# Preparing modulation, context and the first tokens by feature block in a hybrid recurrent trunk on one core

## The chip, the core and the metric

The kernel runs on one core of one Trainium2 chip. Its engines run side by side, each on an instruction list of its own: TensorE (PE; its weight loads are listed as PEld), VectorE (DVE), ScalarE (ACT), GpSimd (POOL) and SyncE (SP). SP and ACT also issue DMA transfers, in the order of their lists. The metric is the device time of one execution in microseconds. Three runs of the kernel before gave a median of 2798.66 us (2794.95 to 2799.27).

## The reference, cut to what matters

One layer: an HGRN2 gated recurrence over 2048 latent tokens of 1024 features, preceded by 256 context tokens that share all weights, then a gated ConvFFN. The change lies in the first steps, the modulated norm and the projections of the first head.

```python
sc_lat, sc_ctx = jax.nn.silu(c), jax.nn.silu(c_ctx)
m_l = (sc_lat @ w_ada[l] + b_ada[l])[:, None, :]
m_c = sc_ctx @ w_ada[l] + b_ada[l]
sh1, sc1, g1, sh2, sc2, g2 = jnp.split(m_l, 6, axis=-1)
csh1, csc1, ... = jnp.split(m_c, 6, axis=-1)
hl = modulate(rmsnorm(lat, norm_g[l, 0]), sh1, sc1)     # h * (1 + scale) + shift
hc = modulate(rmsnorm(cx, norm_g[l, 0]), csh1, csc1)
# in the mixer, for context and latents alike, 8 heads of 128:
q, zf_fwd, zf_bwd, v, g = jnp.split(h @ w_in, 5, axis=-1)
q = silu(q)
f = lb[d] + (1.0 - lb[d]) * sigmoid(zf)                  # per direction d
logf, k = log(f), 1.0 - f
# chunkwise scan of each direction: S_t = diag(f_t) S_{t-1} + k_t v_t^T, o_t = S_t^T q_t
# the latent scans start from the context's final state
out = (rmsnorm(o, g_gain) * silu(g)) @ w_out
```

After the mixer come the residual, the second modulated norm, the ConvFFN (a depthwise convolution of width 3 between two large products) and the final norm.

## The kernel before, in words

**Number format.** Large products are made from two-term splits: `split` (L76) writes a rounded high part with an ACT copy (L77) and the remainder with a DVE subtraction (L78). A product is then three matmuls (high x high, high x low, low x high).

**Modulation rows (L196 to L220).** The first 2048 columns of w_ada give shift and scale. SP and ACT load them as 16 blocks of 128 x 1024 (0.5 MB each) into four large places of SBUF; later the tokens live in the same places (`place`, L133). Per block two float32 matmuls (L205) with the two silu columns of c and c_ctx as weights write 2 x 512 values into four banks. Each such matmul shows as two instructions in the trace, 64 in all. ACT copies the four banks (L212), 16 small transposes (L215) turn the rows into columns, and DVE makes A1 (scale) and B1 (shift), for latents and context.

**Tokens.** A tile is 128 tokens of 1024 features. `load_x` (L175) loads it (L163) and `normalize` (L93) scales it: a square with sum on ACT (L97), a small DVE operation (L73), a power on POOL (L74), the scaling on ACT (L100). `transpose_mod` (L104) turns four blocks of 128 features on TensorE (L109) into one bank and modulates each on ACT (L113) or DVE (L116), 128 x 128 at a time; `put_tok` (L146) splits the half tile into its place. Two context tiles and token tile 0 are made so at once (L221 to L229). Tiles 1 to 7 follow by `make_tok` (L383), one tile after another through one bank.

**Heads.** Half of the tokens (tiles 0 to 7, two units of four tiles) go through all eight heads, then the other half. `head` (L702) runs for each head: three context projections, of the two gates and the values (L714), and for each unit five projections (two gates, query, value, output gate). A projection (`acc`, L367) has eight steps, one for each block of 128 features, of three matmuls each (L372 to L374), 512 columns wide for a unit and 256 for the context. `gates`, `factors`, `values` and `unit_steps` (L402 to L616) make the scan's factors on ACT, DVE and POOL, and the scores, states and outputs with small matmuls (L503 to L602).

**Order.** The program is traced in the order of the source, and a scheduler with a cost model puts each engine's instructions in a fixed list, mostly in that order, taking ready work earlier where an engine would sit idle. An agenda written by hand (`at`, `tick`, L353 to L365) puts side work behind the n-th projection step: tiles 1 to 4 at steps 2 to 18, tiles 5 to 7 from step 20 on (L773 to L778). `issue_after` puts instructions behind a given one on the same engine's list. A buffer with few copies makes the next user's load wait until the last reader is through; raw weight blocks have two (`rawp`), split weights four (`wp`).

In the first head unit 0's gates, query and value are projected, then unit 1's gates, query and value, then both output gates (L744 to L754).

Of the kernel before, what the change touches and what calls it, by code (L numbers as in the profile page):

```python
# [11 lines left out]
F32 = mybir.dt.float32  # L12
# [33 lines left out]
def body(ctx, tc, a, out):  # L46
# [29 lines left out]
    def split(h, l, src):  # L76
        act.activation(h, src, AF.Copy)  # L77
        dve.tensor_tensor(l, src, h.bitcast(F32), OP.subtract)  # L78
# [67 lines left out]
    def put_tok(hm, t, kh):  # L146

        src = hm[:, 4 * kh:4 * kh + 4]
        j = t % UT
        if t < 0:  # L150
            b = cxt[:, kh, t + 2]
            split(b[:, 0], b[:, 1], src)
        elif t < HT:
            b = block(t // UT, kh)[:, j]
            split(b[:, 0], b[:, 1], src)
        else:
            b = xp.tile([128, 2, 4, 128], F32R, name="stg", tag="stg", bufs=1)
            split(b[:, 0], b[:, 1], src)
            sp.dma_start(tok_d[t // UT - 2][kh][:, j], b.bitcast(F32))
# [15 lines left out]
    def load_x(xt, t, hm=None):  # L175
        x_tile(xt, t)
        junk = hm.rearrange("p k n -> p (k n)") if hm is not None else \
            xp.tile([128, D], F32, name="junk", tag="stg", bufs=1)
        normalize(xt, junk, gp, on_act=True)


    HEAD0 = (2, 1, 3, 0)
    staged = {}
    with ExitStack() as c0:
        p0s = pool_(c0, "p0s", space=PSUM)
        silv = sil.rearrange("p (two k) -> p k two", two=2)
        mps = [p0s.tile([2, 512], F32, name=f"mps{n}") for n in range(4)]
        ada = [place(i, [128, 4, D], F32, "wada") for i in range(4)]

        def early_x(t):  # L190

            tag = ("ke", "ke", "kd", "qp", "qp", "qi", "qi")[t + 2]
            staged[t] = gp.tile([128, D], F32, name="x0", tag=tag, bufs=1 if tag == "kd" else 2)
            load_x(staged[t], t)

        act.activation(sil, vec[:, V_C:V_C + 16], AF.Sigmoid)  # L196
        dve.tensor_tensor(sil, sil, vec[:, V_C:V_C + 16], OP.mult)
        for k in range(KT):
            for i in range(2):
                n = 2 * k + i  # L200
                wt = ada[n // 4][:, n % 4]
                (sp if i else act).dma_start(
                    wt, a["w_ada"][k * 128:(k + 1) * 128, i * D:(i + 1) * D])
                for n in range(2):
                    pe.matmul(mps[2 * i + n], silv[:, k, :], wt[:, n * 512:(n + 1) * 512],  # L205
                              start=k == 0, stop=k == KT - 1)
            if 3 <= k < 6:
                early_x(k - 5)
        head0 = {ty: load_w(0, ty) for ty in HEAD0[:2]}
        m2 = [gp.tile([2, 512], F32, name="m2", tag="qg"[n // 2], bufs=2) for n in range(4)]  # L210
        for n in range(4):
            ada_done = act.activation(m2[n], mps[n], AF.Copy)  # L212
        mt = p0s.tile([128, 16, 2], F32, name="mt")
        for j in range(16):
            pe.transpose(mt[:, j, :], m2[j // 4][:, j % 4 * 128:(j % 4 + 1) * 128],  # L215
                         ident[0:2, 0:2])
        for i in (1, 0):
            dve.tensor_tensor(B1[i], mt[:, 0:8, i], vec[:, V_BA:V_BA + 8], OP.add)
            dve.tensor_tensor(A1[i], mt[:, 8:16, i], vec[:, V_BA + 8:V_BA + 16], OP.add)
            dve.scalar_tensor_tensor(A1[i], A1[i], 1.0, vec[:, V_NG:V_NG + 8], OP.add, OP.mult)  # L220
        hms = [new_hm(),  # L221
               xp.tile([128, KT, 128], F32, name="hm", tag="xt", bufs=1),
               gp.tile([128, KT, 128], F32, name="hm", tag="S", bufs=1)]
        for g in range(2):
            for j, hm in enumerate(hms):
                t = j - 2
                m = 0 if t >= 0 else 1
                transpose_mod(staged[t], hm, g, p0s, A1[m], B1[m], "tr", 3, (g + j) % 2)
                put_tok(hm, t, g)  # L229
        with tc.issue_after(ada_done.ins):  # L230
            head0.update({ty: load_w(0, ty) for ty in HEAD0[2:]})
            for t in range(1, 5):
                early_x(t)
# [75 lines left out]
    def mixer_scan():  # L309
# [56 lines left out]

        def acc(z, w, rs):  # L367

            for k in range(KT):
                r = rs[k // 4]  # L370
                h, l = r[:, :, 0, k % 4], r[:, :, 1, k % 4]
                pe.matmul(z, w[:, 0, k], h, start=k == 0, stop=False, skip_group_check=True)  # L372
                pe.matmul(z, w[:, 0, k], l, start=False, stop=False, skip_group_check=True)  # L373
                pe.matmul(z, w[:, 1, k], h, start=False, stop=k == KT - 1, skip_group_check=True)  # L374
                tick()
# [7 lines left out]
        def make_tok(t, xt=None):  # L383

            got = [xt]
            hms = []
# [6 lines left out]
            def put(g):  # L393
                if not hms:
                    hms.append(new_hm())
# [1199 lines left out]
```

## Time and profile before

| | |
|---|---|
| Median of three runs | 2798.66 us |
| The profiled execution | 2798.74 us, its span 2797.0 us |
| TensorE busy | 2732.9 us (98% of the span) |
| DVE, ACT, POOL busy | 1977.5, 1147.7, 571.9 us |
| DMA | 402.18 MB, mean 144 GB/s |
| Granted clock of TensorE | 0.99 mean |

Rows of a table of stretches give start and end, the length, then for each engine its busy time and number of instructions, then TensorE's granted clock (1.00 is full), the share of time that the DMA engines were busy, and GB/s. Rows of the order in time give start, length, engine, line and operation, what is written from what, the shape, and in brackets how long the engine had been idle and what ended that. Rows of groups give busy time and the mean length of one instruction in ns, then the idle time in front of them. A matmul's length is its own, from entering to leaving; in a stream the next enters before it, so a stream's price is read from start to start. Rows of waits give total, count and the longest.

### The profile page before, as it was taken

To read this page: it belongs to the slowest core of one execution; us is meant where nothing else is said; L and a number is where in the kernel's file an instruction comes from. 1 tells how busy PE (TensorE), PEld (TensorE's weight loads), DVE (VectorE), ACT (ScalarE), POOL (GpSimd) and SP (SyncE) were. 2 spreads that over 40 slices of the span, in tenths; PEclk is the share of its full clock that TensorE was granted. 3 is DMA by queue.
4 is the path that set the end of the run, shared out by engine and by line. 5 is a ranking of instruction groups with operands and counts; after the bars stand their busy time and mean duration, and the time that the engine had idled before them with its cause. 6 is when DMAs were issued, how large, how long until landed. Compare 5 with 4: busy or idle time off the path is not lost. (4 is left out here: it accounts for less than half of the span.)

```text
span 2797.0 us, 42007 instructions
## 1 busy us (share of the span) xinstructions
PE 2732.9 (98%) x16072; PEld 2269.1 (81%) x16072; DVE 1977.5 (71%) x2804; ACT 1147.7 (41%) x1908; POOL 571.9 (20%) x882
## 2 busy tenths in 40 slices
PE   7899999999999999998999999999999999999998
PEld 3688888888888888886887788888888888887887
DVE  3665556657575775567887877887877787576886
ACT  5423343323233332324666444444444444333343
POOL 2211111111111111111120443432344430000001
PEclk9999999999999999998999999999999999999999
DMA  5122333215442432236888422226222223987663
GB/s 227 54 62 86 95 114 100 86 54 172 165 129 71 129 106 76 84 110 233 284 306 309 149 85 81 91 91 266 95 90 77 91 91 122 328 290 242 197 195 121
DMA packets 226161, 402.18 MB, mean 144 GB/s; under 512 B 29220, under 2 KB 136612, under 8 KB 222120
## 3 DMA queue, kind: packets, MB, share of 16 engines
q1 hardware_dynamic: 221928, 390.79, 42.0%
q10 hardware_dynamic: 4032, 8.72, 0.8%
q8 instruction: 126, 2.06, 0.3%
q14 instruction: 75, 0.61, 0.1%
HBM read 289.04 MB, written 110.38 MB: 143 GB/s over the span
## 5 line engine op out<-in xcount | busy, mean ns | idle before, releaser
L372 PE MATMUL z<-tok,w 128*128 128x512 f32 x1280 | 516.4, 404 | 0.0
L374 PE MATMUL z<-tok,w 128*128 128x512 f32 x1280 | 502.5, 393 | 0.0
L373 PE MATMUL z<-tok,w 128*128 128x512 f32 x1280 | 501.5, 392 | 0.0
L78 DVE TENSOR_TENSOR w<-raw,w 128x512 fp32r<-128x512 f32 (+1 forms) x260 | 239.6, 925 | 146.8 <-ACT w L77 142.8
L374 PEld LDWEIGHTS z<-tok,w 128*128 128x128 f32 x1280 | 241.3, 189 | 51.2
L372 PEld LDWEIGHTS z<-tok,w 128*128 128x128 f32 x1280 | 242.3, 189 | 47.3 <-issue 3.5
L373 PEld LDWEIGHTS z<-tok,w 128*128 128x128 f32 x1280 | 242.1, 189 | 44.5
L77 ACT ACTIVATE w<-raw 128x512 fp32r<-128x512 f32 (+1 forms) x260 | 196.1, 760 | 134.0 <-PE zd L857 77.4
L1427 PE MATMUL y<-wd,ml 128*128 128x512 f32 x600 | 234.8, 391 | 3.7 <-DVE ml L78 3.7
L1425 PE MATMUL y<-wd,mh 128*128 128x512 f32 x600 | 234.1, 390 | 1.2 <-ACT X L1460 1.2
L1426 PE MATMUL y<-wd,mh 128*128 128x512 f32 x600 | 233.9, 390 | 0.0
L426 DVE TENSOR_TENSOR_SCAN S<-F,d 128x528 f32<-128x528 f32 (+1 forms) x80 | 91.6, 1145 | 99.9 <-ACT F L409 99.3
L78 DVE TENSOR_TENSOR w<-s,w 128x512 fp32r<-128x512 f32 x126 | 121.0, 965 | 54.5 <-ACT w L77 53.7
L854 PE MATMUL zc<-rT,w 128*128 128x512 f32 x352 | 137.1, 390 | 1.2 <-DVE uv L1312 1.0
L857 PE MATMUL zc<-rT,w 128*128 128x512 f32 x352 | 136.9, 389 | 0.0
L856 PE MATMUL zc<-rT,w 128*128 128x512 f32 x352 | 136.9, 389 | 0.0
L1427 PEld LDWEIGHTS y<-wd,ml 128*128 128x128 f32 x600 | 113.0, 188 | 29.0 <-DVE ml L78 5.8
L77 ACT ACTIVATE w<-s 128x512 fp32r<-128x512 f32 x126 | 78.3, 628 | 138.8 <-POOL s L910 82.2
L1425 PEld LDWEIGHTS y<-wd,mh 128*128 128x128 f32 x600 | 113.1, 188 | 25.0 <-ACT X L1460 1.7
L459 POOL COPY TX<-S 128x4 f32<-128x4 f32 x32 | 25.1, 784 | 529.0 <-DVE S L426 529.0
L1426 PEld LDWEIGHTS y<-wd,mh 128*128 128x128 f32 x600 | 112.9, 188 | 23.7
L854 PE MATMUL za<-rB,w 128*128 128x512 f32 x336 | 130.7, 389 | 0.0
(339 smaller groups left out, 6334.1 us busy)
## 6 DMA issues: line engine op xcount, KB each, us to landing
raw<-in_w_up_dram SPq DMA_DIRECT2D x88, 512.0 KB, 3.9
raw<-in_w_in_dram SPq DMA_DIRECT2D x80, 512.0 KB, 3.8
lr<-m SPq DMA_DIRECT2D x49, 512.0 KB, 5.7
m<-r SPq DMA_DIRECT2D x66, 256.0 KB, 4.2
spare<-in_w_ada_dram SPq DMA_DIRECT2D x32, 512.0 KB, 4.5
kq<-stash SPq DMA_DIRECT2D x15, 1024.0 KB, 7.8
og<-stash SPq DMA_DIRECT2D x28, 512.0 KB, 5.2
u<-in_w_down_dram SPq DMA_DIRECT2D x51, 256.0 KB, 3.9
```

The lines of the kernel that those rows point to most:

```text
L77: act.activation(h, src, AF.Copy)
L78: dve.tensor_tensor(l, src, h.bitcast(F32), OP.subtract)
L372: pe.matmul(z, w[:, 0, k], h, start=k == 0, stop=False, skip_group_check=True)
L373: pe.matmul(z, w[:, 0, k], l, start=False, stop=False, skip_group_check=True)
L374: pe.matmul(z, w[:, 1, k], h, start=False, stop=k == KT - 1, skip_group_check=True)
L426: dve.tensor_tensor_scan(flat(S[:, d]), flat(F[:, d]), flat(d1[:, 0:ns]), 0.0, OP.mult, OP.max)
L854: pe.matmul(o, w[:, 0, k], r[:, :, 0, k], start=start and k == 0, stop=False, skip_group_check=True)
L856: pe.matmul(o, w[:, 0, k], r[:, :, 1, k], start=False, stop=False, skip_group_check=True)
L857: pe.matmul(o, w[:, 1, k], r[:, :, 0, k], start=False, stop=k == 3, skip_group_check=True)
L1425: pe.matmul(z, lh, rh, start=start, stop=False, skip_group_check=True)
L1426: pe.matmul(z, lh, rl, start=False, stop=False, skip_group_check=True)
L1427: pe.matmul(z, ll, rh, start=False, stop=stop, skip_group_check=True)
```

## The change

**Rows.** The silu columns are copied into a zeroed tile `silp` of 32 columns per feature block. For each block k four matmuls write 32 partitions each of one bank `mp`: shift in two halves, scale in two halves. One ACT copy and four transposes of 128 x 128 follow. Two w_ada blocks (k of 6 and 7) move from SP's queue to ACT's. Raw weights of the two gates are loaded between the w_ada blocks, those of value and query behind the first two token tiles.

**Context.** Both context tiles are normalized with the scaling on DVE (`on_act` is left out) and transposed before the modulation rows are ready, into four banks of two feature blocks by two tiles. Modulation is then 128 x 256 at a time, and each quarter is split at once.

**Tokens of units 0 and 1.** All eight tiles are loaded into buffers of their own (`stage`), which later serve the scan, and normalized in place with a common junk tile. `unit_tok` transposes one feature block of all four tiles of a unit into one of three banks in turn, modulates 128 x 512 at a time (even blocks on ACT, odd ones on DVE) and splits. Three blocks of unit 0 stand in the third context projection. Then both gates of unit 0 advance together, block by block, each step followed by the block three ahead; the agenda puts the squares of tiles 4 to 7 and the blocks of unit 1 among these steps and the query's. `make_tok` is left for the other half's tiles.

```diff
     def split(h, l, src):
-        act.activation(h, src, AF.Copy)
-        dve.tensor_tensor(l, src, h.bitcast(F32), OP.subtract)
+        i = act.activation(h, src, AF.Copy)
+        j = dve.tensor_tensor(l, src, h.bitcast(F32), OP.subtract)
+        return i.ins, j.ins
+    @contextmanager
+    def behind_of(pair):
+        with tc.issue_after(pair[0]), tc.issue_after(pair[1]):
+            yield
...
+    def stage(t):
+        tag = ("ke", "ke", "qp", "qp", "qi", "qi", "xt", "hm", "stg", "raw")[t + 2]
+        p = {"xt": xp, "hm": xp, "stg": xp, "raw": rawp}.get(tag, gp)
+        staged[t] = p.tile([128, D], F32, name="x0", tag=tag, bufs=1 if p is xp else 2)
+        x_tile(staged[t], t)
+    def turn_tok(tp, ts, ks):
+        for i, k in enumerate(ks):
+            for j, t in enumerate(ts):
+                pe.transpose(tp[:, i, j], staged[t][:, k * 128:(k + 1) * 128], ident)
+    def modulated(hm, tp, k, m, on_act):
+        if on_act:
+            act.activation(hm, tp, AF.Identity, bias=B1[m][:, k:k + 1], scale=A1[m][:, k:k + 1])
+        else:
+            dve.tensor_scalar(hm, tp, A1[m][:, k:k + 1], B1[m][:, k:k + 1], OP.mult, OP.add)
...
+        pool.memset(silp, 0.0)
+        for k in range(2):
+            ada_load(act, k, 0)
+            ada_load(sp, k, 1)
         act.activation(sil, vec[:, V_C:V_C + 16], AF.Sigmoid)
         dve.tensor_tensor(sil, sil, vec[:, V_C:V_C + 16], OP.mult)
+        dve.tensor_copy(silp[:, :, 0:2], silv)
+        stage(-2)
+        stage(-1)
+        for k in range(2, KT):
+            ada_load(act, k, 0)
+            ada_load(act if k >= 6 else sp, k, 1)
+            if k in (4, 5):
+                head_raw[6 - k] = raw_w(6 - k)
+        stage(0)
+        stage(1)
+        for t in (-2, -1):
+            normalize(staged[t], junk, gp)
+        late_junk = place(2, [128, D], F32, "junk")
...
         for k in range(KT):
+            if k == 5:
+                for g in range(4):
+                    turn_tok(tps[g], (-2, -1), (2 * g, 2 * g + 1))
+            for c in range(4):
+                n = 2 * k + c // 2
+                pe.matmul(mp[32 * c:32 * c + 32], silp[:, k],
+                          ada[n // 4][:, n % 4, c % 2 * 512:(c % 2 + 1) * 512],
+                          start=k == 0, stop=k == KT - 1, skip_group_check=True)
+        split_head0(2, head_raw[2])
+        act.activation(m2, mp, AF.Copy)
+        for j in range(4):
+            pe.transpose(mt[:, j], m2[:, j * 128:(j + 1) * 128], ident)
...
+        for g in range(4):
+            hm = gp.tile([128, 2, 2, 128], F32, name="hm", tag="g", bufs=2)
             for i in range(2):
+                modulated(hm[:, i], tps[g][:, i], 2 * g + i, 1, i == 0)
+            b = cxt[:, g // 2, :, :, 2 * (g % 2):2 * (g % 2) + 2]
+            made = split(b[:, :, 0], b[:, :, 1], hm.rearrange("p k s n -> p s k n"))
+            if g == 1:
+                split_head0(1, head_raw[1])
+                with behind_of(made):
+                    normalize(staged[0], late_junk, gp)
+        head_raw[3] = raw_w(3)
+        stage(2)
+        stage(3)
+        head_raw[0] = raw_w(0)
+        for t in range(4, 8):
+            stage(t)
+        with behind_of(made):
+            normalize(staged[1], late_junk, gp)
+            split_head0(3, head_raw[3])
+            for t in (2, 3):
+                normalize(staged[t], late_junk, gp)
...
+        places = ("kv", "o", "tr")
+        def unit_tok(u, k):
+            tp = ps.tile([128, 1, UT, 128], F32, name="tp", tag=places[k % 3], bufs=1)
+            turn_tok(tp, range(UT * u, UT * u + UT), (k,))
+            hm = gp.tile([128, UT, 128], F32, name="hm", tag="g", bufs=2)
+            modulated(hm, tp[:, 0], k, 0, k % 2 == 0)
+            b = block(u, k // 4)[:, :, :, k % 4]
+            return split(b[:, :, 0], b[:, :, 1], hm)
...
                 ckd, csd = factors(h, None, None, None)
+                if first:
+                    made_tok = []
+                    for k in range(3):
+                        at(clock[0] + 2 * k, lambda k=k: made_tok.append(unit_tok(0, k)))
                 cv, turn = values(project(weight(3), None), 2)
...
             if first:
-                gate(0)
+                zs = [ps.tile([128, UT, 128], F32, name="z", tag="pj", bufs=3) for _ in range(2)]
+                def more(t):
+                    with behind_of(made_tok[-1]):
+                        normalize(staged[t], late_junk, gp)
+                for i in range(UT):
+                    at(clock[0] + 1 + 2 * i, lambda i=i: more(UT + i))
+                for k in range(KT):
+                    at(clock[0] + 10 + 2 * k, lambda k=k: unit_tok(1, k))
+                for k in range(KT):
+                    for d, z in enumerate(zs):
+                        step(z, weight(2 - d), block(0, k // 4), k)
+                    if k + 3 < KT:
+                        made_tok.append(unit_tok(0, k + 3))
+                    if k == 3:
+                        split_head0(0, head_raw[0])
+                for d, z in enumerate(zs):
+                    gates(d, h, 0, z)
                 query(0, 24)
...
-        for t in range(1, 5):
-            for i, f in enumerate(make_tok(t, staged[t])):
-                at(2 + 4 * (t - 1) + 2 * i, f)
-        for t in range(5, 8):
-            for i, f in enumerate(make_tok(t)):
-                at(20 + 10 * (t - 5) + 3 * i, f)
```

More of the change, by code (lines that the diff above doesn't have):

```diff
@@ L146, in put_tok @@
     def put_tok(hm, t, kh):
[L148 to L159, printed above, removed]
+        b = xp.tile([128, 2, 4, 128], F32R, name="stg", tag="stg", bufs=1)
+        split(b[:, 0], b[:, 1], hm[:, 4 * kh:4 * kh + 4])
+        sp.dma_start(tok_d[t // UT - 2][kh][:, t % UT], b.bitcast(F32))
     def x_tile(xt, t):
@@ new lines, in ada_load, with raw_w, split_head0 @@
+        def ada_load(q, k, i):
+            n = 2 * k + i
+            q.dma_start(ada[n // 4][:, n % 4], a["w_ada"][k * 128:(k + 1) * 128, i * D:(i + 1) * D])
+        def raw_w(ty):
+            raw = rawp.tile([128, D], F32, name="raw", tag="raw")
+            sp.dma_start(raw, a["w_in"][0, ty])
+            return raw
+        head0 = {}
+        def split_head0(ty, raw):
+            head0[ty] = w = wp.tile([128, 2, KT, 128], F32R, name="w", tag="w")
+            split(w[:, 0], w[:, 1], raw.rearrange("p (k n) -> p k n", k=KT))
@@ L209, in body @@
[L209 to L220, printed above, removed]
```

85 lines of the change are left out of this document (34 added, 51 removed).

## The prediction

> **What bounds the kernel now.** I read the page first, then the table of stretches, then TensorE's order of time over the first 235 us, then the groups by shape and the chain of waits there. The page:
>
> ```profile
> span 2797.0 us, 42007 instructions
> ...
> PE   7899999999999999998999999999999999999998
> ...
> PEclk9999999999999999998999999999999999999999
> ```
>
> TensorE is full in all slices but the first two (70 us each). So the kernel is a string of TensorE work, and what shortens the start moves everything behind it. The diff touches only the start. Stretches (us, then busy time of PE, PEld, DVE, ACT, POOL, then granted clock, DMA share, GB/s):
>
> ```profile
> 0.00:10.00 10.00, 4.84 (x8) 0.82 (x9) 0.52 (x4) 1.50 (x2) 5.78 (x10) 1.00 0.81 297
> 10.00:20.00 10.00, 10.00 (x25) 2.01 (x24) 1.23 (x5) 2.30 (x3) 6.82 (x22) 1.00 1.03 411
> 20.00:30.00 10.00, 10.00 (x25) 1.98 (x24) 0.31 (x2) 5.30 (x7) 1.08 (x2) 1.00 1.03 412
> 66.00:109.00 43.00, 34.09 (x243) 27.14 (x242) 26.63 (x51) 22.49 (x42) 8.55 (x15) 0.90 0.10 31
> 109.00:154.00 45.00, 43.37 (x299) 35.76 (x298) 23.60 (x34) 17.28 (x30) 6.56 (x13) 0.94 0.27 83
> 167.00:233.00 66.00, 66.00 (x513) 55.59 (x512) 39.14 (x57) 19.16 (x32) 10.25 (x24) 1.00 0.18 53
> 45.70:49.10 3.40, 3.39 (x16) 3.10 (x15) 2.65 (x6) 3.21 (x6) 1.05 (x2) 0.50 0.87 308
> 107.20:114.00 6.80, 6.04 (x19) 4.97 (x20) 3.33 (x7) 3.39 (x8) 0.00 (x0) 0.50 0.25 77
> ```
>
> TensorE's marks (start, length, instruction):
>
> ```profile
> 5.16 29.11 PE L205 MATMUL mps<-wada,sil 128*2 128x512 f32 x64 [5.16 <-DVE sil L197]
> 40.24 0.39 PE L372 MATMUL z<-cxt,w 128*128 128x256 f32 x1 [0.17 <-ACT cxt L77]
> 51.85 0.60 PE L109 MATMUL tp<-ident,x 128*128 128x128 f32 x4
> 52.20 0.36 PE L374 MATMUL z<-cxt,w 128*128 128x256 f32 x1
> 54.55 0.28 PE L372 MATMUL z<-cxt,w 128*128 128x256 f32 x1
> 55.51 0.28 PE L374 MATMUL z<-cxt,w 128*128 128x256 f32 x1
> 65.88 1.63 PE L372 MATMUL z<-tok,w 128*128 128x512 f32 x3
> 108.72 1.63 PE L372 MATMUL z<-tok,w 128*128 128x512 f32 x3
> 147.74 0.32 PE L547 MATMUL sc<-qm,km 128*32 128x64 f32 x8
> 148.73 0.36 PE L547 MATMUL sc<-qp,ke 128*32 128x32 f32 x16
> 152.96 0.39 PE L372 MATMUL z<-tok,w 128*128 128x512 f32 x1
> 153.41 0.39 PE L374 MATMUL z<-tok,w 128*128 128x512 f32 x1
> 166.21 0.40 PE L372 MATMUL z<-tok,w 128*128 128x512 f32 x1
> 232.53 0.28 PE L372 MATMUL z<-cxt,w 128*128 128x256 f32 x1
> ```
>
> Read them as milestones: modulation rows done at 34.3, context projections 40.2 to 55.8, first gate at 65.9, unit 1's first gate at 108.7, first head done at 153.6. From first gate to end the first head takes 87.8 us; the second does the same ten projections in 66.3 (166.2 to 232.5), TensorE full. A projection step costs 0.225 us per 512-column matmul (152.96 to 153.41 is two) and 0.12 per 256-column one (54.55 to 55.51 is eight); four transposes hold the queue 0.35 (51.85 to 52.20). From 66 to 109 TensorE is busy 34.1 of 43 us. Who makes TensorE wait, and for what:
>
> ```profile
> PE tp L109 <- ACT xt L100: 5.9, 3, 2.3
> PE tp L109 <- DVE hm L116: 5.7, 3, 2.7
> ACT tok L77 <- DVE hm L116: 10.5, 5, 2.9
> ```
>
> So it is the preparation of tokens, tile by tile in one bank, that starves TensorE. Prices of its operations and of those that replace them:
>
> ```profile
> L113 ACT ACTIVATE hm<-tp,B,A 128x128 f32<-128x128 f32 x40 | 15.2, 460 | 4.7 <-PE tp L109 4.5
> L116 DVE TENSOR_SCALAR hm<-tp,A,B 128x128 f32<-128x128 f32 x40 | 13.6, 404 | 5.1 <-PE tp L109 5.0
> L78 DVE TENSOR_TENSOR tok<-hm,tok 128x512 fp32r<-128x512 f32 x16 | 10.9, 684 | 12.5 <-ACT tok L77 12.5
> L77 ACT ACTIVATE tok<-hm 128x512 fp32r<-128x512 f32 x16 | 10.1, 634 | 10.6 <-DVE hm L116 10.5
> L97 ACT ACTIVATE junk<-x 128x1024 f32<-128x1024 f32 x7 | 7.5, 1067 | 13.4 <-DMA x<-in_ctx_dram 12.5 <-DMA x<-in_x_dram 0.7 <-ACT junk L97 0.2
> L77 ACT ACTIVATE w<-raw 128x1024 fp32r<-128x1024 f32 x9 | 9.5, 1058 | 2.7 <-DMA raw<-in_w_in_dram 2.7
> L74 POOL TENSOR_TENSOR rs<-rs,mhalf 128x1 f32<-128x1 f32 x11 | 5.9, 543 | 56.8 <-DVE rs L73 56.8
> L505 ACT ACTIVATE kt<-tr 128x512 f32<-128x512 f32 x5 | 3.0, 597 | 3.3 <-PE tr L503 3.3
> L409 ACT ACTIVATE F<-F,lb,oml 128x512 f32<-128x512 f32 x4 | 3.3, 814 | 0.1
> L646 DVE TENSOR_SCALAR acc<-spare,sil x4: 731/746/753, 647.2 to 1028.3; 128x1024 f32<-128x1024 f32 x4
> ```
>
> **The change part by part.** I carry the milestones through.
>
> *Rows in four column groups.* 32 matmuls (64 instructions) stay, but four with weights of 32 columns write four partition groups of one bank. Before, 64 instructions took 29.1 us (0.455 each), one after the other, and that, not the transfers, set 34.3. No row shows 512-column groups side by side. The nearest is L547, which writes 32-row groups: 96 instructions stand from 147.74 to 149.09, 14 ns each. One alone shows about 0.2 us, but they are pipelined, so I don't take the whole ratio. Bounds: a quarter of 29.1 (7.3 us) and the whole of it. I take the quarter, since L547 is the same form. Then the last block of w_ada decides. Ahead of it now stand 16 blocks of w_ada, two context tiles and two of w_in, 20 of 0.524 MB: 10.5 MB. By 20 us 2.97+4.11 MB have moved; the rest at 412 GB/s is done at 28.3, and about 1 us more to land. Four last matmuls, 0.9 us, or twice that at half clock: rows at 30.8 (high bound: 34.3 plus 16 context transposes now put inside, 1.4 us at about 0.09, 35.7). The widened silu tile (one memset on POOL, one small DVE copy) lies under the wait for the first block and costs nothing; without that cover, 0.5 us. Two w_ada blocks move from SP to ACT's queue; behind them there stand only the context's squares, which are needed at the sixth of eight steps, in the shadow of the transfers.
>
> *Context by blocks.* One copy of the rows (0.6, as the L505 row) in place of four, then four transposes, three small DVE operations and hand-overs, which I estimate at 1.8 together (twice the 0.35 above for cold transposes, the rest for the others): 33.2. Then four quarters, each a modulation on ACT (about 0.46) beside one on DVE, ACT copy 0.63, DVE subtraction 0.69. ACT spends 1.1 per quarter, so TensorE may start at 34.5 against 40.2. After the second quarter one token square (1.25 with its read-out) is put into ACT's line. Last quarter: 33.2+4.4+1.25+0.7 = 39.6. Two further projections of 24 x 0.12 = 2.9 and three sets of transposes of 0.36: 46.7. Against it 1.7 us, if 3.4 us fall into half clock as at 45.7 before: 48. Before 55.8.
>
> *First gate.* It needs four token tiles normalized, then a block through transpose, modulation, copy, subtraction. ACT's line from 30.8: row copy 0.6, idle 1.8, quarters 4.4, four squares 5.0, one split of w_in 1.06, two context gates 2.0 (half of L505 and L409 and a little, twice): 45.6. Normalizing leaves ACT (1.15 each) for DVE, 0.75 by the L646 row, behind POOL's 0.54. Then 0.36+0.75+0.63+0.69 and gaps: 49. The transfers do not hold this: tile 3 is the 25th block, 13.1 MB, in by 36 at 412 GB/s. SP's queue is held at the third w_in block until the first split frees its buffer; behind it stand tiles 2 and 3, the fourth block and tiles 4 to 7. That split is ready at 21 to 24 us, so 10 us of cover; without it each late us is one at the gate. Before 65.9.
>
> *The gate pass step by step.* Both gates advance by feature block, two matmul triples (1.35) and four transposes (0.36): 1.7 us of TensorE per block. ACT has per block a copy 0.63 and every other time a modulation (bounds 0.60, the L505 row, and 0.81, L409; I take 0.7): 1.0; DVE the same with 0.69+0.35. For the two units, 16 modulations of 512 columns (11 us over both engines) replace 64 of 128 (64 x 0.43 = 27.5). But into the same pass go four squares (5.0), a split (1.06), the remaining context work (2) and the first blocks of unit 1: ACT 16.5 us until block 7 is done, more than TensorE's 13.6. ACT sets the pass. 49+16.5+1.4 = 67; I take 70, as an order of hand-overs never fills an engine. Query and value, 5.4 each with unit 1's other transposes 1.4, plus turns: unit 1's gates start at 83.5 against 108.7. The junk tile shares its place with unit 1's first block, which so waits for the last square (about 58): no cost.
>
> *The rest of the head* is unchanged: 108.7 to 153.6, 44.9, of which 6.8 at half clock. Bounds 41.5 and 46; I take 45: end at 128.5.
>
> **Sum.** 153.6-128.5 = 25 us. The profiled execution took 2798.7 us (1.7 beside its span), as the median does: 2798.7-25 = 2774. Nothing later gives it back: weights come through the same two buffers relative to TensorE, and 167 to 233 is full.
>
> **A rule weighed.** At 45.7 and 107.2 the granted clock was 0.50 after stretches in which TensorE had pauses. The Trainium skill, "TensorE: Matmul & The Clock Gate", Part 1, says that the array idles at half rate and needs about 3.4 us of sustained work to be let go; the 3.4 us row agrees. By that rule the modulation rows, now sparse, leave the array cold where before it was kept warm by 29 us of matmuls: it speaks against the change. It would give the second rival.
>
> **The rivals.** *First: the blocks hand over badly.* Each engine has one fixed order. If TensorE meets the transposes in the third context projection before the tiles are normalized (3 us) and a block costs its chain, 0.36+0.7+0.63+0.69 and four gaps, 3.2 us instead of 2.1, the pass grows by 9: gain 13, 2786. For it: L77 waited 10.5 us for L116 before. Against: three banks. *Second: half clock* in context and gate pass, 72 x 0.1 plus 20 of the 48 x 0.22 not under ACT: some 9 us, 2783. *Third: the column groups run in series*, rows at 35.7: 2779. *Fourth, better:* TensorE as full as in the second head, 49+66.3+5.8 = 121: 2766. *Slower: no overlap of blocks at all.* Place: the 16 blocks between 49 us and unit 1's gate. With squares and splits (6 us) inside, that gate starts at 55 + 16 blocks; from 3.4 us per block it is later than 108.7. At 3.7 it is 114, +5.5, 2804. For it: the chain is 2.4 plus gaps and an in-order queue of TensorE stands behind each block's transposes; against: blocks use different engines and three banks in turn. That the change does nothing (rows hidden, tokens still the limit): within 5 us, 2797.
>
> **How the numbers follow.** Forecast 0.45; first 0.16, second 0.08, third 0.06; fourth 0.14; slower 0.06; nothing 0.05. The range, 2762 to 2789, goes from all engines full (2766, less 4 for the bound of 41.5) to the first rival and its bound. What a measurement can tell from no change is 0.2%, 5.6 us: faster 0.89, same 0.05, slower 0.06.
>
> **What would show it.** Rows done near 31 and waiting for transfers, not TensorE; first context matmul near 34.5; first gate near 49, ended by ACT's copy; both gates done by 70; unit 1's gate near 83; the second head beginning near 128. Wrong, if the row matmuls take over 25 us, if ACT idles over 5 us between 49 and 70 while TensorE waits, or if the second head's stretch grows beyond 66 us.

## The result, and the profile after

Measured side by side, the kernel after takes 2775.45 us (median; 2774.19 to 2777.47), the kernel before 2797.38 us (2794.95 to 2799.27). The ratio is 0.9923 with a 95% interval of 0.9906 to 0.9940: 21.9 us less. The profiled execution took 2775.32 us. Where a difference to "after" is given below, it is one between medians; each kernel's interval is against before, so that a difference to after of less than some 5 us rests on the trace beside it.

The page of the kernel after (the span in 40 equal slices, as before):

```profile
span 2773.6 us, 41929 instructions
...
PE   6999999999999999998998999999999999999998
...
PEclk8999999999999999998999999999999999999999
```

The first two slices were 7 and 8 and are 6 and 9: TensorE does less in the first 70 us, and is over 90% busy in the second 70. TensorE's order of time, its marks (start, length, instruction, and in brackets how long it had been idle and what ended that):

```profile
19.32 1.94 PE L250 MATMUL mps<-wada,silp 128*32 128x512 f32 x8 [0.62 <-DMA wada<-in_w_ada_dram]
27.00 4.95 PE L250 MATMUL mps<-wada,silp 128*32 128x512 f32 x20 [3.19 <-DMA wada<-in_w_ada_dram]
40.42 0.58 PE L425 MATMUL z<-cxt,w 128*128 128x256 f32 x1 [5.80 <-DVE hm L196]
49.37 0.33 PE L190 MATMUL tp<-ident,x 128*128 128x128 f32 x1 [0.20 <-DVE x L108]
52.91 0.39 PE L425 MATMUL z<-tok,w 128*128 128x512 f32 x1
83.74 0.39 PE L425 MATMUL z<-tok,w 128*128 128x512 f32 x1
113.25 0.73 PE L666 MATMUL o<-states,qi 128*128 128x128 f32 x2 [3.66 <-DVE states L644]
131.17 0.40 PE L427 MATMUL z<-tok,w 128*128 128x512 f32 x1
132.21 0.36 PE L425 MATMUL z<-cxt,w 128*128 128x256 f32 x1
```

Against before, in us from the start of the span:

| | before | after | forecast |
|---|---|---|---|
| modulation rows done | 34.3 | 31.95 | 30.8 |
| first context matmul | 40.2 | 40.4 | 34.5 |
| first gate | 65.9 | 52.9 | 49 |
| both gates of unit 0 done | 82.8 | 72.5 | 70 |
| unit 1's first gate | 108.7 | 83.7 | 83.5 |
| first head done | 153.8 | 131.6 | 128.5 |
| end of the span | 2797.0 | 2773.6 | |

The last step of the two gates waits for block 7's copy on ACT, and its last matmuls leave at 72.5:

```profile
70.26 0.30 PEld L425 LDWEIGHTS z<-tok,w 128*128 128x128 f32 x2 [0.26 <-ACT tok L77]
...
71.87 0.62 PE L427 MATMUL z<-tok,w 128*128 128x512 f32 x2
```

By the count of matmuls, two steps of the query stand ahead of that (from 64.2 on), so TensorE had work all the same.

Of the 23.4 us of the two spans 22.2 are there when the first head ends, and what follows takes 2642.0 us instead of 2643.2. The rest is told by the stretches (start and end, length, busy time of PE, PEld, DVE, ACT, POOL, clock, DMA share, GB/s):

```profile
52.91:70.60 17.69, 17.35 (x98) 13.56 (x97) 11.10 (x22) 12.54 (x23) 2.16 (x4) 1.00 0.01 2
70.60:83.74 13.14, 13.14 (x68) 10.89 (x67) 11.86 (x17) 10.20 (x17) 3.74 (x12) 1.00 0.24 80
14.40:31.50 17.10, 10.30 (x44) 1.57 (x44) 2.95 (x5) 3.25 (x5) 2.68 (x8) 0.50 1.03 410
38.30:45.10 6.80, 4.68 (x22) 4.68 (x23) 5.91 (x12) 5.56 (x10) 0.91 (x2) 0.50 0.53 211
113.40:116.80 3.40, 3.40 (x13) 3.01 (x14) 0.65 (x2) 2.17 (x4) 0.00 (x0) 0.51 0.41 119
```

From 52.9 to 83.7 TensorE is busy 30.5 of 30.8 us at full clock. Before, from 66 to 109, it was 34.1 of 43. From unit 0's first gate to unit 1's it is 30.8 us instead of 42.8: 12.0 us of the gain. Another 13.0 are there when the first gate starts, and 2.8 are lost again between unit 1's first gate and the end of the first head. The last three rows are the stretches at half clock. The waits of TensorE in the first 135 us (total, times, longest) have changed places:

```profile
PE mps L250 <- DMA wada<-in_w_ada_dram: 9.1, 5, 4.4
PE z L425 <- DVE hm L196: 5.8, 1, 5.8
PE mps L250 <- DVE silp L227: 5.1, 1, 5.1
PE o L666 <- DVE states L644: 3.7, 1, 3.7
PE tp L190 <- DVE x L108: 0.5, 2, 0.3
```

Of the waits for tokens (5.9 and 5.7 us before the longest two) 0.5 us is left. The rows wait for transfers, the context's first product for the end of the last quarter's modulation, and one matmul late in the head for the states.

### The profile page after: what moved, and what is told of

It reads as the page before. It is cut to its first block, busy times and chain, and to the rows that moved or that the text cites. A ratio compares the mean times of both kernels' runs of the same rounds, so it can differ in the third digit from the quotient of the medians.

```text
span 2773.6 us, 41929 instructions
## 1 busy us (share of the span) xinstructions
PE 2713.4 (98%) x16060; PEld 2259.2 (81%) x16060; DVE 1978.4 (71%) x2787; ACT 1125.9 (41%) x1867; POOL 566.9 (20%) x883
## 5 line engine op out<-in xcount | busy, mean ns | idle before, releaser
L425 PEld LDWEIGHTS z<-tok,w 128*128 128x128 f32 x1280 | 240.8, 188 | 47.8 <-issue 3.5
L78 DVE TENSOR_TENSOR w<-s,w 128x512 fp32r<-128x512 f32 x126 | 121.5, 970 | 53.0 <-ACT w L77 52.2
L935 PE MATMUL za<-rB,w 128*128 128x512 f32 x336 | 130.7, 389 | 0.0
L937 PE MATMUL za<-rB,w 128*128 128x512 f32 x336 | 130.7, 389 | 0.0
```

The source lines that it names most:

```text
L78: j = dve.tensor_tensor(l, src, h.bitcast(F32), OP.subtract)
L935: pe.matmul(o, w[:, 0, k], r[:, :, 0, k], start=start and k == 0, stop=False, skip_group_check=True)
L937: pe.matmul(o, w[:, 0, k], r[:, :, 1, k], start=False, stop=False, skip_group_check=True)
```

## The experiments

The theory after the result: the gain is the tokens' preparation by blocks, which keeps TensorE fed from the first gate to unit 1's; the 2.3 us won at the rows are lost again at the wait of 5.8 us. The rival: the column groups, or the clock, carry the gain.

### Parts undone and parts alone

*Tokens tile by tile again*, everything else as after:

```diff
-for k in range(KT):
-    for d, z in enumerate(zs): step(z, weight(2 - d), block(0, k // 4), k)
-    if k + 3 < KT: made_tok.append(unit_tok(0, k + 3))
+for i in range(2 * UT):
+    at(clock[0] + 8 + 2 * i, lambda i=i: unit_half(UT + i // 2, i % 2))
+gate(0)
```

> Rows in column groups and the context by quarters stay as after; the tokens of the first two units go back to one tile at a time through one bank with modulations of 128 columns, and the first gates stand one after the other. Theory (the gain is the preparation of tokens by blocks): the first gate falls from 52.9 back to about 62, unit 1's gates from 83.7 to 100 to 106, and the kernel takes 2789 to 2797 us, so three quarters or more of the 22 us are gone. Rival (the rows and the context carry the gain): the first gate moves by less than 4 us and the kernel takes less than 2781 us.

Measured: 2789.03 us, 13.6 more than after. TensorE's waits over the first 135 us, and two stretches (columns as above):

```profile
PE tp L463 <- DVE hm L196: 8.7, 6, 2.1
...
PE tp L463 <- ACT hm L194: 4.9, 3, 1.7
```

```profile
53.00:72.00 19.00, 7.92 (x28) 5.63 (x29) 8.64 (x19) 9.42 (x22) 0.00 (x0) 0.53 0.00 0
72.00:90.00 18.00, 17.29 (x85) 13.69 (x84) 12.96 (x27) 13.03 (x26) 3.48 (x6) 0.92 0.10 30
```

The first gate falls back to 70.4, unit 1's gates to 101.6, and TensorE is idle for more than half of the first stretch, at half clock. The first gate was expected at 62, but comes later even than before (65.9). So the blocks carry 13.6 of the 21.9 us, some 60% and not three quarters. The figure holds for this placing: all half tiles of unit 0 stand in the third context projection, where in the kernel before the first tile was made ahead. The edit also sets the two gates one after the other, which by itself costs nothing that the times show (below). What is left, 8.4 us, is what rows, context, normalizing and the early loads bring with tokens made tile by tile; the context by quarters and the early loads weren't taken out by themselves.

*The column groups alone*, put into the kernel before:

```diff
-mps = [p0s.tile([2, 512], F32, name=f"mps{n}") for n in range(4)]
+silp = gp.tile([128, KT, 32], F32, name="silp", tag="kt", bufs=2)
+mp = p0s.tile([128, 512], F32, name="mps")
...
+pe.matmul(mp[32 * c:32 * c + 32], silp[:, k], wt[:, n * 512:(n + 1) * 512], ...)
```

> The kernel before with the modulation rows in four column groups and nothing else. Theory: the rows end at about 31 to 32 instead of 34.3, the first gate comes 0 to 3 us earlier, unit 1's gates are still limited by the tile-by-tile preparation, and the kernel takes 2794 to 2798 us. Rival (the rows carry the gain): 2785 us or less. If leaving the array cold costs something, 2798 to 2802 us.

Measured: 2795.03 us, ratio to before 0.9993 (0.9983 to 1.0003), so not told apart from no change. The interval leaves room for a gain of up to some 5 us, and in the traced execution, 2.4 us below the median, the first head ends at 149.2 instead of 153.8. The rows are done at 29.1, earlier than expected, but the first context matmul stays at 40.2 and the first gate comes at 64.1 instead of 65.9, because the tile-by-tile chain is next in line (TensorE waits 3.16 us for the modulation there):

```profile
27.99 1.06 PE L209 MATMUL mps<-wada,silp 128*32 128x512 f32 x8
...
33.59 2.20 PE L109 MATMUL tp<-ident,x 128*128 128x128 f32 x8 [3.16 <-ACT hm L113]
```

*The groups in series*, in the kernel after:

```diff
+silp = wp.tile([128, 96 + KT * 128], F32, name="silp", tag="w")
-pe.matmul(mp[32 * c:32 * c + 32], silp[:, k], ...)
+pe.matmul(mp, silp[:, 96 + 128 * k - 32 * c:224 + 128 * k - 32 * c], ...)
```

> The kernel after with the modulation rows' four groups in series again: the same 32 matmuls and the same transfers, but each over all 128 columns, so TensorE is busy and warm to the end of the rows. Theory (the first gate is set by normalizing, and the rows' end by transfers): rows end at 34 to 36 instead of 31.95, no half clock in the context, first gate within 2 us of 52.9, kernel 2775 to 2779 us. Rival (column groups are worth their whole 7 to 22 us of TensorE): 2782 us or more. Third (the cold array is what costs): the kernel gains, 2772 us or less.

Measured: 2785.3 us, 9.9 more than after: the rival's case, and a miss for the theory. TensorE's order of time there:

```profile
5.07 11.21 PE L250 MATMUL mps<-wada,silp 128*128 128x512 f32 x20 [5.07 <-DVE silp L227]
16.64 8.85 PE L250 MATMUL mps<-wada,silp 128*128 128x512 f32 x20 [0.36 <-DMA wada<-in_w_ada_dram]
...
28.15 1.86 PE L190 MATMUL tp<-ident,x 128*128 128x128 f32 x15 [2.54 <-DVE x L108]
29.84 10.46 PE L250 MATMUL mps<-wada,silp 128*128 128x512 f32 x24
...
48.16 0.55 PE L425 MATMUL z<-cxt,w 128*128 128x256 f32 x1 [6.51 <-DVE hm L196]
```

The rows end at 40.3 and not at 34 to 36: TensorE has no slack any more, so the slow first 20 (2.4 us more than the next 20), the wait of 2.54 us for the second context tile and the 1.9 us of transposes put among the rows all come on top. Everything behind shifts with them, the first gate by 7.9 us (60.8). So the column groups are worth about 10 us beside the blocks and at most some 5 without them: the parts do not add up, as each is worth its whole only where the other doesn't bind.

*The gates one after the other*, and *one bank for the blocks*:

```diff
-for k in range(KT):
-    for d, z in enumerate(zs):
+for d, z in enumerate(zs):
+    for k in range(KT):
         step(z, weight(2 - d), block(0, k // 4), k)
```

> The kernel after with its first two gates one after the other instead of step by step: the first carries all the blocks' preparation. Theory: in the first gate TensorE has only 0.7 us of matmuls per block beside 0.36 us of transposes, so the hand-over of a block over ACT and DVE sets it, at about 1.6 to 2 us per block against 1.1 of TensorE; the first projection grows by 3 to 6 us, and the kernel takes 2778 to 2782 us. Rival (step by step is worth nothing, the blocks' width and banks are everything): within 1.5 us of after, 2774 to 2777 us.

```diff
-places = ("kv", "o", "tr")
+places = ("tr", "tr", "tr")
```

> The kernel after with all the blocks' transposes through one bank instead of three in turn. Theory: a block then costs its whole turn (transposes 0.36, the modulation 0.7 and the hand-overs) in one bank, about 1.5 us, below the 1.7 us of TensorE per block in the gate pass, so the pass of 19 us grows by 1 to 4 us and the kernel takes 2776 to 2780 us. Rival (the banks are what lets the blocks overlap): the pass grows by 8 us or more, 2784 us or more.

Measured: 2771.15 us with the gates apart (ratio to before 0.9908, 0.9892 to 0.9924), 4.3 *less* than after; 2777.56 us with one bank, 2.1 more; both intervals overlap with after's (0.9906 to 0.9940). With the gates apart the pass does grow (first gate to unit 1's gates 31.9 us instead of 30.8), much less than expected, but the first head ends at 128.5 instead of 131.6. What it wins up to there lies far behind the gates, at the states and in the clock from 90 to 120 us (the second row of that stretch is after's):

```profile
111.64 0.49 PE L666 MATMUL o<-states,qi 128*128 128x128 f32 x2 [1.35 <-DVE states L644]
```

```profile
90.00:120.00 30.00, 28.65 (x237) 23.95 (x237) 20.49 (x29) 10.33 (x18) 4.22 (x12) 1.00 0.30 97
90.00:120.00 30.00, 26.24 (x221) 22.14 (x220) 22.72 (x33) 10.90 (x18) 5.20 (x13) 0.94 0.25 77
```

The wait for the states is 1.4 us instead of 3.7, and the half clock behind it is gone. But the traced execution took 2776.28 us, the longest of its four and no less than after's: what follows the first head took 2646.0 us in it, against 2642.0 after. In the traces of all the runs here that rest lies between 2641.0 and 2646.0 us, so a gain in the whole time isn't shown. Step by step isn't what feeds TensorE, then: it is worth about 1 us up to unit 1's gates. Three banks are worth little: with one, unit 1's gates come 33.3 us after the first gate instead of 30.8, and nearly all of that comes back later in the head (first gate to its end 78.8 us against 78.7).

### The wait for the states

DVE in the kernel after, in order of time:

```profile
111.39 1.22 DVE L517 TENSOR_TENSOR qi<-qp,TB 128x1024 f32<-128x1024 f32 x1
112.52 0.41 DVE L517 TENSOR_TENSOR qm<-qp,TX 128x256 f32<-128x256 f32 x1
112.86 0.34 DVE L644 SCALAR_TENSOR_TENSOR states<-Sf,sd,kv 128x128 f32<-128x128 f32 x1
```

```profile
100.00:110.00 10.00, 9.59 (x49) 7.79 (x47) 10.00 (x15) 1.54 (x2) 2.41 (x10) 1.00 0.13 40
```

The state that TensorE waits for takes 0.34 us, but stands in DVE's list behind the factors of unit 1; DVE is busy 10.00 of 10 us from 100 to 110. The experiment puts the finishing steps of unit 0 six projection steps later:

```diff
-finish(0, (10, 14, 18))
+finish(0, (16, 20, 24))
```

> The kernel after with the three steps that finish unit 0 of the first head (states, outputs) put six projection steps later. Theory (the 2.8 us by which the rest of the head was longer than forecast is TensorE's wait for the states at 113.25 and the 3.4 us of half clock behind it): that wait of 3.7 us and the half clock go, head 0 ends 3 to 5 us earlier, kernel 2770 to 2773 us. Rival (DVE is the limit there, full from 100 to 110, so the wait turns up elsewhere): within 1.5 us of after, or later by up to 3 us.

Measured: 2771.39 us, 4.1 less than after (ratio to before 0.9909, 0.9895 to 0.9922); the first head ends at 126.9. Its DVE from 100 to 110 us, and its TensorE at the states:

```profile
100.00:110.00 10.00, 10.00 (x50) 8.44 (x49) 10.00 (x16) 2.14 (x3) 2.40 (x10) 1.00 0.17 52
```

```profile
113.41 0.49 PE L666 MATMUL o<-states,qi 128*128 128x128 f32 x2 [0.80 <-DVE states L644]
```

DVE is as full as in after and makes the state no earlier (113.0 against 112.9): the rival's premise holds, but not its conclusion. TensorE only meets the wait later, after other work, and so stays at full clock. The stretch from unit 1's gates to the end of the head is 43.7 us instead of 47.8.

### What holds the first gate

The wait of 5.8 us ahead of the context could be for a bank of PSUM or for the data. A first attempt turned the order in which the quarters use their banks:

```diff
+tps = [tps[i] for i in (3, 1, 2, 0)]
```

> The kernel after with one difference: the bank that the first context projection takes over is used by the first quarter's transposes instead of the last's. Theory (TensorE's 5.8 us wait ahead of the first context matmul is the wait for that bank): the first context matmul comes at 36 to 38 instead of 40.4; the first gate moves by less than 1.5 us, since tile 3's normalizing at 49.3 sets it; the kernel takes 2774 to 2776 us. Rival (the wait is for the quarters' data): the first context matmul stays at 40 and nothing moves. Third (the context was the path to the first gate): the first gate comes 3 us earlier and the kernel takes 2771 to 2773 us.

Measured: 2776.02 us, and the same wait of 5.8 us at 39.8. It decides nothing: the wait would stay the same if the banks were given out in the order of use, so that the last quarter had that bank again. No view of the trace names the banks. The second attempt moves the quarters by one bank:

```diff
+mt = p0s.tile([128, 4, 128], F32, name="mt")
 tps = []
 ...
-mt = p0s.tile([128, 4, 128], F32, name="mt")
```

> The kernel after with one difference: the small tile of the rows' transposes is allocated ahead of the quarters' tiles, which moves these by one bank each, so that the bank which the first context projection takes over is the first quarter's and not the last's. (In the earlier attempt the order of use changed, and the allocator followed it: the last quarter had that bank again.) Theory (TensorE's wait of 5.8 us is for that bank): the first context matmul comes at 36 to 38, the wait falls to 2 to 3 us; the first gate stays within 1 us, since tile 3 is normalized no earlier; kernel 2774 to 2776 us. Rival (the wait is for the last quarter whatever the bank): the first context matmul stays at 40. Third (the context carries the first gate): first gate 3 us earlier, kernel 2771 to 2773 us.

Measured: 2774.64 us (0.8 less than after). TensorE starts the context 4.1 us earlier and then waits for data:

```profile
36.35 0.39 PE L425 MATMUL z<-cxt,w 128*128 128x256 f32 x1 [1.68 <-ACT cxt L77]
```

So the 5.8 us were for the bank, and they cost nothing by themselves: the first gate comes at 53.0, as after. The theory's second half falls with that. The other candidate is the line of work ahead of tile 3, in which the split of a weight stands that only the query needs (its first step at 64.2):

```diff
-    if k == 3: split_head0(0, head_raw[0])
+    if k == 3:
+        with behind_of(made_tok[-1]): split_head0(0, head_raw[0])
```

> The kernel after with the split of head 0's last weight (1.04 us of ACT at 44.0, 1.22 us of DVE at 45.1) held back behind the first blocks of tokens, so that the squares and normalizing of tiles 2 and 3 stand ahead of it. Theory (the first gate is set by the line of ACT and DVE work ahead of tile 3's normalizing): tile 3 is normalized 1 to 2 us earlier, the first gate comes at 51 to 52 and the kernel takes 2773 to 2775 us. Rival (the third context projection, in whose queue the blocks' transposes stand, sets the first gate): the first gate moves by less than 0.4 us. Third: the split is late where it went, and the kernel loses 1 us or more.

Measured: 2775.58 us, no gain. In DVE's order of time in the kernel after, two splits stand ahead of the scaling of tile 2 (46.75) and tile 3 (48.55):

```profile
43.71 1.22 DVE L78 TENSOR_TENSOR w<-raw,w 128x1024 fp32r<-128x1024 f32 x1
...
45.10 1.22 DVE L78 TENSOR_TENSOR w<-raw,w 128x1024 fp32r<-128x1024 f32 x1
46.75 0.75 DVE L108 TENSOR_SCALAR x<-x,rs 128x1024 f32<-128x1024 f32 x1 [0.43 <-POOL rs L74]
...
48.55 0.75 DVE L108 TENSOR_SCALAR x<-x,rs 128x1024 f32<-128x1024 f32 x1 [0.37 <-POOL rs L74]
```

With the second of them held back tile 3 is scaled 1.1 us earlier, but the first gate comes at 53.1:

```profile
47.41 0.75 DVE L108 TENSOR_SCALAR x<-x,rs 128x1024 f32<-128x1024 f32 x1 [0.72 <-POOL rs L74]
```

The rival is right here: TensorE itself, late with the context and at half clock from 39.4 to 46.2, needs until then for its three projections. From there to unit 1's gates it is 32.1 us instead of 30.8, so something is lost behind the gate. That the context and tile 3 are two limits, of which each hides the other, is argued so far; the second combination below tests it.

*The array kept busy through the rows*:

```diff
+if k < 7:
+    for c in (512, 256):
+        pe.matmul(dm[:, 0:c], ident, ada[k // 2][:, 2 * k % 4, 0:c], start=True, stop=True)
```

> The kernel after with two further matmuls (512 and 256 columns, full array, into a bank that nothing reads) behind the row matmuls of each of the first seven feature blocks, to fill TensorE's waits for w_ada; they are extra work and are left out of the result. The scheduler also puts the second weight's split ahead of the rows' copy here. Theory (the half clock from 14 to 31 us delays the end of the rows by about 1.5 us, and the half clock from 38 to 45 costs the context little, since it waits for tokens): clock 1.00 through the rows, rows end at 30 to 30.6, first gate 1 to 2 us earlier, kernel 2773 to 2775 us. Rival (the cold array costs the whole start): first gate 4 us earlier or more, 2771 us or less. Third (the array stays cold as long as it has pauses): half clock as in after, rows end at 33 or later, kernel 2776 to 2778 us.

Measured: 2779.96 us, 4.5 more than after, and none of the three expectations held in full:

```profile
19.16 1.14 PE L251 MATMUL mps<-wada,silp 128*32 128x512 f32 x8
20.23 1.56 PE L256 MATMUL dm<-wada,ident 128*128 128x512 f32 x4
```

```profile
10.00:35.00 25.00, 22.58 (x99) 7.76 (x98) 5.00 (x10) 4.30 (x6) 7.04 (x23) 1.00 1.03 411
```

The clock stays at 1.00 from 10 to 35 us, and eight row instructions take 1.14 us instead of 1.94. But rows and extra work together take 2.6 us of TensorE per feature block, as long as its two transfers, so that TensorE never makes up what it is behind, and the rows end at 35.4. From there to the first gate it is 20.3 us against 21.0 after, and TensorE, waiting 6.5 us for the bank, falls to half clock again from 40.1 to 46.9. What the half clock costs the rows in the kernel after isn't measured by this: an upper bound is 2.3 us, from its last 20 instructions at 1.05 instead of 1.94 per eight.

### Together

Two combinations were run. The first turned the quarters' banks as in the first attempt, put the second weight's split, which stood at the second quarter, ahead of the rows' copy, and took the later finish:

```diff
+tps = [tps[i] for i in (3, 1, 2, 0)]
+split_head0(1, head_raw[1])
-finish(0, (10, 14, 18))
+finish(0, (16, 20, 24))
```

> The kernel after with the bank's order, the split of the second head-0 weight ahead of the rows' copy, and the later finish of unit 0 together. Theory: with the context no longer late and the split out of the way, tile 3 is normalized about 1 us earlier; first gate 51 to 52, the wait for the states gone; kernel 2768 to 2772 us. Rival (the edits undo each other, DVE and ACT having no room left): 2774 us or more.

Measured: 2773.59 us, 2.2 more than the later finish alone, with overlapping intervals (0.9901 to 0.9928 against 0.9895 to 0.9922). The wait for the states is down to 0.8 us, but the first gate comes at 53.7: the scheduler now put the context's 16 transposes ahead of the four of the rows, which come at 34.1 instead of 32.7:

```profile
31.98 2.27 PE L190 MATMUL tp<-ident,x 128*128 128x128 f32 x16
...
34.10 0.60 PE L260 MATMUL mt<-ident,m 128*128 128x128 f32 x4
```

The second took both limits off the first gate and the finish later:

```diff
+mt = p0s.tile([128, 4, 128], F32, name="mt")
-    if k == 3: split_head0(0, head_raw[0])
+    if k == 0:
+        with behind_of(made_tok[2]): split_head0(0, head_raw[0])
-finish(0, (10, 14, 18))
+finish(0, (16, 20, 24))
```

> The kernel after with three edits: the rows' transposes take a bank ahead of the quarters' (the first context projection then gets a bank that is free early), the split of head 0's last weight is held behind the third block of tokens, and the finish of unit 0 comes six projection steps later. Theory (the first gate is set twice, by TensorE's late start of the context and by tile 3's normalizing, so that either edit alone moved nothing; the states' wait is a matter of the agenda): first gate at 51 to 52 instead of 52.9, no wait of more than 1 us for the states, no half clock at 113, head 0 ends at 125 to 126.5 instead of 131.6; kernel 2768 to 2771 us. Rival (what is won at the first gate is lost in the gate pass, as the split adds DVE work there): 2771 to 2773 us, no better than the later finish alone.

Measured: 2769.71 us (2767.81 to 2773.12), ratio to before 0.9901 (0.9885 to 0.9918), the lowest median of all. The first gate comes at 50.9 and the first head ends at 125.6:

```profile
50.90 0.39 PE L425 MATMUL z<-tok,w 128*128 128x512 f32 x1
```

The rows were done at 31.25 in this execution; from there the first gate is 19.7 us away, against 21.0 in each of after and the two runs with one edit. So the edits move the first gate by 1.3 us together, where each alone moved it by nothing (with the split held at another place here than in the run alone). But it doesn't last to unit 1's gates:

```profile
83.40 0.39 PE L425 MATMUL z<-tok,w 128*128 128x512 f32 x1
```

They come 32.5 us after the first gate instead of 30.8, and 52.2 us after the end of the rows, against 51.8 in after and with the later finish alone. On this point the rival is right: what is won at the first gate is lost in the pass. From unit 1's gates to the end of the head it is then 42.2 us, TensorE busy in all of it, against 43.7 with the later finish alone, TensorE busy 42.7 and waiting 0.8 for the states; which of the edits brings that, no run shows. Against after the median is 5.7 us lower and against the later finish alone 1.7; the intervals overlap in both cases, and the traced execution took 2773.12 us, more than the 2771.33 of the later finish's. A gain over the later finish alone isn't shown.

## Why the prediction was right, and where it was not

The time forecast was 2774, the measured one 2775.45 us, and the mechanism that carries it was the one named: blocks in place of tiles keep TensorE fed, and nothing behind the first head gives the gain back. That the number fits so well is in part luck: of its gain of 25 us the sum had 16.9 up to the first gate, 8.3 from there to unit 1's gates and nothing in the rest of the head; the traces show 13.0, 12.0 and a loss of 2.8. Inside, five steps were off, and two of them cancelled.

- *Rows.* "I take the quarter" and "then the last block of w_ada decides" held: 20 instructions in 4.95 us, 0.25 each at half clock against 0.455 in series, and 9.1 us of waiting for transfers, all of it before 27.0. The end was 1.1 us late: the last weight load that waited for a transfer went at 29.6, and TensorE, which ran those 20 instructions without a pause at half clock, then had 2.4 us left where the sum had 0.9, or twice that.
- *Column groups in series*, the third rival, was priced at 2779 us with rows at 35.7; the run gave 40.3 and 2785. The terms left out were TensorE's wait for the second context tile, which then lies on the path, and the slow first 20 instructions.
- *First context matmul.* "TensorE may start at 34.5" failed by 5.9 us: the step took the data as the only condition and forgot the bank, held by the last quarter. It had no price of its own in the end.
- *First gate at 49, ended by ACT's copy.* It came at 52.9, straight behind a context projection, whose matmuls the sum had done by 48. I had added up ACT's line to 45.6; tile 3 was scaled at 49.3, because DVE's two weight splits of 1.22 us and POOL's step stood in its chain, and behind the transposes that projection had 3 us left, which I had not counted. With tile 3 scaled 1.1 us earlier the gate came no sooner, so TensorE's own line, 5.9 us late at the context and 6.8 us at half clock, was as long. The first rival's condition (transposes met before the tiles are normalized) held here with 0.2 us of waiting instead of 3.
- *"ACT sets the pass", 21 us.* Right only for the gates' end: their last step waits for ACT's copy of block 7 (70.3), and they are done at 72.5, 19.6 us after they began, two steps of the query included. TensorE does not wait with them. In the first 17.7 us it is busy 17.35, and ACT 12.54. The sum had put a split and all eight blocks into ACT's line there; the split (44.0) and the copies of the first two blocks (50.5 and 51.5) came ahead of the gate. And it had not counted on steps of the query and transposes of unit 1 filling the gap. So unit 1's gates came at 83.7 against 83.5 forecast: a start 3.9 us late and a way to them 3.7 us shorter cancelled.
- *The rest of the head, 45.* It took 47.8. The sum took this stretch over unchanged, but a fuller DVE made the state later than TensorE asked for it: 3.7 us of waiting and 3.4 us at half clock. With the finish later it is 43.7.
- *The slower rival* (no overlap of blocks, from 3.4 us per block) was far off: from 52.9 to 83.7 the list shows one wait of TensorE for tokens, of 0.3 us. *Half clock*, the second rival, came in the rows and the context and not in the gate pass (1.00), and did not decide. The Trainium skill, "TensorE: Matmul & The Clock Gate", Part 1, was weighed for that; its window of about 3.4 us agrees with the stretches here (3.4 us and multiples of it).
- *Slips in the working*, without weight for the forecast: 39.6, 5.8 and 1.1 are 46.5 and not 46.7; the second rival's terms come to 11.6 us, or 9.9 without the 1.7 already in the sum, and not 9; and of the half clock from 107.2 to 114.0 before, 5.3 and not 6.8 us lie behind 108.7.

## What to carry to other kernels

Price a change of order by who is next in line: column groups gave 10 us where the tokens were ready for it and at most some 5 where they weren't, and 1.3 us that two edits won together at one gate were gone by the next. Ask of each early start not only for its data but for the bank it writes to, and where a short instruction stands in a full engine's list, try to move its reader later: that was enough here (moving the writer earlier wasn't tried). When a stretch is taken over as unchanged, look at what the change puts into the lists of the other engines there.

## What the hardware showed that was not expected

- Four float32 matmuls with 32 weight columns each, into four partition groups of one bank, run side by side almost completely: eight instructions in 1.05 to 1.14 us at full clock, against 0.455 us each in series in the kernel before, 3.2 to 3.5 times as fast. The Trainium skill, "TensorEngine Tiling (Array Packing)", Theoretical Speedup, states up to 4 times for 32 columns; the trace comes near it.
- TensorE was held at half clock for 17.1 us in a stretch in which it was busy 10.3 us by the rows' own lengths, with pauses of 0.6 to 4.4 us; in the run with extra work, busy 22.6 of 25 us, it stayed at 1.00. The half-clock stretches in the first 135 us of the kernel after last 17.1, 6.8 and 3.4 us: multiples of 3.4.
